# Squares moved to ScalarE, VectorE's order written out and a third weight's low part made by DMA, in the first stage of a two-layer decoder trunk

## The chip, the cores and the metric

The kernel runs on one core of one Trainium2 chip. The time is device microseconds (us) for one execution of the whole program; three executions of the kernel before took 2656.12, 2658.39 and 2658.79 us, median 2658.39. Engine names as in the profile: PE is TensorE (matrix multiply) and PEld its weight load, DVE is VectorE, ACT is ScalarE, POOL is GpSimd, SP is SyncE, whose queue issues most DMA transfers.

## The reference, cut to what matters

Two layers (`DEPTH = 2`) of a hybrid block on one sequence of 1024 tokens of width 1024, all in float32:

```python
for l in range(DEPTH):
    h = rmsnorm(x, norm_mix[l])
    proj = einsum('btd,de->bte', h, w_in[l])
    q, k, v, u, ug, ga, gb = split(proj, SPLITS, axis=-1)   # 1024, 128, 128, 512, 512, 1024, 1024 wide
    a_out = sliding_window_attention(partial_rope(rmsnorm(q)), partial_rope(rmsnorm(k)), v, sinks[l])
    c_out = conformer_conv(u, ug, ...)        # GLU, causal depthwise convolution of width 31, LayerNorm, silu, projection
    x = x + (sigmoid(ga) * a_out + sigmoid(gb) * c_out) @ w_out[l]
    g, up = split(rmsnorm(x, norm_ffn[l]) @ w_gate_up[l], 2)
    x = x + (silu(g) * up) @ w_down[l]
```

## The kernel before, in words

The activations lie transposed: 8 tiles of 128 channels x 1024 tokens. Each float32 operand of a matrix product is split in two numbers, a rounded high part (`hx`, `wh`) and the low rest (`lx`, `wl`), and a product is the three terms `wh*hx + wh*lx + wl*hx` (`mm3`, L245 to L251). A term on 1024 tokens is a pair of matmuls of 128x512. One k-step of one weight tile is three such pairs, in the order hx,wh, then lx,wh, then hx,wl, so the low part of the weight is wanted only by the third pair.

RMSNorm is not applied to the input before the product. The tile x is scaled by the norm's weight and split (`split_g`: ACT makes `hx`, DVE makes `lx`), and the factor per token, 1/rms, is multiplied into the results later. For it, the squares of the 8 input tiles are added up in `acc` (`sumsq`), a row of 16 tiny matmuls (`tokmean`, `pss` in the rows) sums `acc` over channels, POOL raises to the power -1/2 (`rtok`), DVE spreads it on a diagonal (`dg`) and two matmuls (`pb`) broadcast it to the tile `R`.

The first stage of a layer projects K and V together (8 k-steps of six pairs), then `u0`, the first convolution tile (third weight), then `ug0`, `q0` and so on in the order of `INPROJ`. In layer 1 (`l == 0`) the program starts with nothing on the chip: the eight input tiles `xi` and the weights arrive by DMA during the K and V steps. In layer 2 the input is already split when K and V begin.

Weights are fetched ahead by `fetch`: a DMA on SP's queue brings the raw tile, ACT casts it to `wh` (L134), `low` makes `wl`. There are two ways for that. While `spaced[0]` is false, POOL subtracts, `wl = raw - wh` (L141). When it is true, ACT writes `wl = -wh` (L144) and an accumulating DMA on POOL's queue adds the weight from memory to it (L145). `spaced[0]` is set after the K and V steps. Tiles of `wl` come from two buffers (`WLO = 2`), so the third weight's `wl` takes the buffer of the first one (K's).

The order of PE's instructions is the order of the code (`MAN`). DVE's is that of the code from the K results on (`dve`); in the head of the program the order on ACT, DVE and POOL is chosen by a list scheduler from its estimate of times. Pending pieces such as `norm_a` are placed by a clock of k-steps (`after`, `tick`): in layer 1 `norm_a` comes two ticks after the K and V loop, which is after the first k-step of `u0`; in layer 2 it comes before it.

The convolution's tile `y` (L510) is 128x1024 float32 with one buffer; it is first written when `ug0` is done.

## Time and profile before

| | us |
|---|---|
| median of three executions (lowest, highest) | 2658.39 (2656.12, 2658.79) |
| the profiled execution | 2658.14 |
| its span, first to last instruction | 2656.4 |
| PE busy in the span | 2562.6 (96%) |
| DVE, POOL, ACT busy | 1785.8, 1423.7, 1152.9 |
| mean granted clock of PE | 0.987 |

The span is cut into stages by times from its start: in layer 1, K and V run from 7.2 to 34 us and u0 from there to 63 us; in layer 2, K and V run from 1343 to 1365 us. A row of the timeline gives start, duration, engine, line, operation, what it writes and reads, and in brackets how long the engine had been idle and what ended that. Busy POOL and DVE times hold waits for each other, as two durations of one instruction show, for instance 1.89 and 2.87 us for the same square.

### The profile page before, as it was taken

The page shows a single profiled execution, that of the slowest core. Times are in us where ns is not written, and L with a number is a line of the kernel's source. Part 1 is how long each engine was busy: PE and PEld are TensorE (multiplying, and loading weights), DVE is VectorE, ACT ScalarE, POOL GpSimd, SP SyncE. Part 2 cuts the span into 40 slices and gives each one's busy share as a digit, 9 for nine tenths or more (in the row PEclk, how much of TensorE's full clock was granted, in tenths as well). Part 3 has the DMA queues.
Part 4 walks back from the last instruction along what each step waited for, and adds up shares of the span by engine and source line. Part 5 has one row for each costly group of instructions (what it writes and reads, how often), then busy time and mean ns, then how long its engine had stood idle before and what let it go on. Part 6 is the DMA issues. An engine that isn't in the chain of part 4 may idle for free.

```text
span 2656.4 us, 33362 instructions
## 1 busy us (share of the span) xinstructions
PE 2562.6 (96%) x11736; PEld 2094.6 (79%) x11736; DVE 1785.8 (67%) x2063; ACT 1152.9 (43%) x2290; POOL 1423.7 (54%) x1004
## 2 busy tenths in 40 slices
PE   7998999999999999999999989999999999999999
PEld 5786877888778888878777778778887788888887
DVE  6688988551667777855637989975516777878344
ACT  3365666632523222344524656666225223233443
POOL 6165565325257767765522655653253667777444
PEclk8999999999999999999999999999999999999999
DMA  4444345675254444476734444456733454446666
GB/s 150 95 100 121 97 107 136 182 248 206 95 182 149 160 167 169 159 275 217 236 96 93 111 111 102 110 148 212 258 143 119 163 178 159 151 167 218 212 226 208
DMA packets 146119, 427.30 MB, mean 161 GB/s; under 512 B 17120, under 2 KB 17376, under 8 KB 145952
## 3 DMA queue, kind: packets, MB, share of 16 engines
q1 hardware_dynamic: 137168, 393.63, 44.0%
q0 software_dynamic: 8640, 31.46, 7.0%
q8 instruction: 92, 1.51, 0.2%
q14 instruction: 75, 0.61, 0.1%
q10 hardware_dynamic: 144, 0.09, 0.0%
HBM read 290.63 MB, written 115.34 MB: 153 GB/s over the span
## 4 chain that ended last, share of the span: by engine, by line
PE 69%; DVE 13%; DMA 6%; ACT 4%; issue 3%; POOL 3%; SPq 1%; DVEq 0%; ACTq 0%; POOLq 0%
PE b L873 43%; PE ps L251 21%; DVE y L515 5%; DMA qs<-q 2%; DMA rot<-q 1%; PE po L721 1%; POOL rot L398 1%; PE pT L691 1%; ACT wh L134 1%; DVE q L412 1%; DVE acc L304 1%; POOL q L397 1%; DMA yd<-y 1%; DVE A L733 1%; DVE mx L671 1%
## 5 line engine op out<-in xcount | busy, mean ns | idle before, releaser
L160 POOL TENSOR_TENSOR plo<-fraw,phi 128x512 fp32r<-128x512 f32 x290 | 425.4, 1476 | 232.8 <-ACT phi L158 219.4
L160 POOL TENSOR_TENSOR plo<-fs,phi 128x512 fp32r<-128x512 f32 x160 | 262.4, 1650 | 252.2 <-ACT phi L158 244.3
L515 DVE SCALAR_TENSOR_TENSOR y<-a,vec,y 128x1024 f32<-128x1024 f32 x240 | 358.4, 1493 | 3.8
L158 ACT CAST phi<-fraw 128x512 fp32r<-128x512 f32 x444 | 257.6, 618 | 235.0 <-POOL plo L160 134.5
L251 PE MATMUL ps<-hx,wh 128*128 128x512 f32 x1056 | 343.2, 406 | 7.2 <-ACT hx L292 7.2
L251 PE MATMUL ps<-hx,wl 128*128 128x512 f32 x1056 | 331.9, 395 | 6.0 <-POOL wl L141 6.0
L251 PE MATMUL ps<-lx,wh 128*128 128x512 f32 x1056 | 332.7, 396 | 0.8 <-DVE lx L293 0.8
L158 ACT CAST phi<-fs 128x512 fp32r<-128x512 f32 x160 | 95.4, 620 | 534.1 <-DVE fs L173 534.1
L160 DVE TENSOR_TENSOR plo<-fraw,phi 128x512 fp32r<-128x512 f32 x154 | 129.4, 847 | 188.7 <-ACT phi L158 186.5
L873 PE MATMUL b<-plo,phi 128*128 128x512 f32 x616 | 240.6, 391 | 5.3 <-DVE plo L160 5.1
L251 PEld LDWEIGHTS ps<-hx,wl 128*128 128x128 f32 x1056 | 201.4, 191 | 50.1 <-POOL wl L141 6.5
L873 PE MATMUL b<-phi,plo 128*128 128x512 f32 x616 | 239.8, 389 | 0.0
L873 PE MATMUL b<-phi 128*128 128x512 f32 x616 | 239.7, 389 | 0.0
L251 PEld LDWEIGHTS ps<-lx,wh 128*128 128x128 f32 x1056 | 202.4, 192 | 47.0 <-DVE lx L293 2.2
L251 PEld LDWEIGHTS ps<-hx,wh 128*128 128x128 f32 x1056 | 191.1, 193 | 42.1 <-ACT hx L292 7.2
L141 POOL TENSOR_TENSOR wl<-raw,wh 128x1024 fp32r<-128x1024 f32 (+1 forms) x40 | 79.9, 1998 | 192.7 <-PE ps L251 176.4
L675 ACT ACTIVATE sc<-sc,nm,fq 128x129 f32<-128x129 f32 x256 | 123.7, 487 | 117.5 <-DVE nm L673 117.2
L134 ACT CAST wh<-raw 128x1024 fp32r<-128x1024 f32 (+1 forms) x100 | 98.0, 980 | 164.8 <-PE ps L251 113.3
L937 DVE TENSOR_TENSOR g<-g 128x512 f32<-128x512 f32 x88 | 105.0, 1193 | 66.4 <-POOL g L941 46.2
L145 POOL DMA_DIRECT2D wl<-win x60 | 53.3, 888 | 177.6 <-ACT wl L144 172.6
L706 POOL TENSOR_SCALAR_AFFINE_SELECT ph<-ph 128x512 fp32r<-128x512 f32 x64 | 69.3, 1083 | 143.0 <-DVE pl L698 143.0
L941 POOL TENSOR_TENSOR g<-g,u 128x512 f32<-128x512 f32 (+1 forms) x84 | 128.6, 1548 | 30.6 <-DVE u L994 24.2
(254 smaller groups left out, 6184.5 us busy)
## 6 DMA issues: line engine op xcount, KB each, us to landing
fraw<-wgu SPq DMA_DIRECT2D x88, 512.0 KB
raw<-win SPq DMA_DIRECT2D x68, 512.0 KB
wl<-win POOLq DMA_DIRECT2D x60, 512.0 KB, 6.4
act<-g SPq DMA_DIRECT2D x44, 512.0 KB
dw<-wdn SPq DMA_DIRECT2D x44, 512.0 KB
td<-g SPq DMA_DIRECT2D x44, 512.0 KB
sd<-dw SPq DMA_DIRECT2D x44, 512.0 KB
fraw<-sd SPq DMA_DIRECT2D x88, 256.0 KB
```

Of the source, the lines that this page charges most:

```text
L134: nc.scalar.copy(wh, raw)
L141: nc.gpsimd.tensor_tensor(out=wl, in0=raw, in1=wh.bitcast(F32), op=ALU.subtract)
L145: nc.gpsimd.dma_start(wl, src, accum_op=ALU.add)
L158: nc.scalar.copy(hi, src)
L160: (eng or nc.gpsimd).tensor_tensor(out=lo, in0=src, in1=hi.bitcast(F32), op=ALU.subtract)
L251: nc.tensor.matmul(ps[:, sl], a[:, wc], b[:, sl], start=first and j == 0, stop=last and j == 2)
L515: nc.vector.scalar_tensor_tensor(out=y, in0=a[:, j:j + T], scalar=V(w0 + j), in1=y, op0=ALU.mult, op1=ALU.add)
L675: nc.scalar.activation(sc[:, n], sc[:, n], AF.Exp, bias=nm[:, n:n + 1], scale=fq[:, 4 * j + n:4 * j + n + 1], accum_out=den[:, n:n + 1])
L706: nc.gpsimd.affine_select(out=src, in_=src.bitcast(F32), pattern=[[0, 4], [-1, P]], compare_op=ALU.is_gt, fill=0.0, base=0, channel_multip ...
L873: nc.tensor.matmul(ps, w[:, ai * P:(ai + 1) * P], x, start=first and j == 0, stop=last and j == 2, skip_group_check=True)
L937: nc.vector.tensor_tensor(out=o, in0=x, in1=y, op=ALU.subtract)
L941: nc.gpsimd.tensor_tensor(out=g[:, sl], in0=g[:, sl], in1=u[:, sl], op=ALU.mult)
```

## The change

Four edits in the head of the program, two of which also hold in layer 2.

1. The squares of the eight input tiles in layer 1 are made by ACT (`AF.Square`) and no longer by POOL; the additions into `acc` stay on DVE.
2. The order on DVE and ACT in the head is that of the code: split of tile e, then square and addition of tile e - 1. The first two weights' high and low parts are made inside that loop (`parts` holds them back until then).
3. `spaced[0]` becomes true before the third weight is prepared, in both layers, so its low part is made by ACT and the accumulating DMA.
4. That low part lies in a tile of the convolution's tag `y` (`spare`), in both layers, and no longer in K's `wl` buffer; the first weight whose `wl` waits for the buffer of one that is used after V is now the sixth, and no longer the fifth. `YB = 1` only names the number of `y` buffers.

```diff
-    def fetch(limit=len(wseq)):
+    spare = []
+
+    def fetch(limit=len(wseq), parts=len(wseq)):
...
-        while given[1] < given[2] and given[1] <= given[0] + AHEAD:
+        while given[1] < min(given[2], parts) and given[1] <= given[0] + AHEAD:
...
-            wl = wp.tile([P, n], F32R, tag="wl", bufs=WLO, name="wl")
+            wl = spare.pop() if spare else wp.tile([P, n], F32R, tag="wl", bufs=WLO, name="wl")
...
-    def sumsq(acc, x, e, first=False, add=None):
+    def sumsq(acc, x, e, add=None):
         sq = acc if e == 0 else t4("sq")
-        if first:
-            nc.gpsimd.tensor_tensor(out=sq, in0=x, in1=x, op=ALU.mult)
-        else:
-            nc.scalar.activation(sq, x, AF.Square)
+        nc.scalar.activation(sq, x, AF.Square)
         if e > 0:
             (add or nc.gpsimd).tensor_tensor(out=acc, in0=acc, in1=sq, op=ALU.add)
...
             with tc.manual_schedule(engines={mybir.EngineType.SP}):
-                fetch(1)
+                fetch(1, 0)
                 for e in range(KD):
                     nc.sync.dma_start(xin[e], xT[e])
                     if e == 0:
-                        fetch(2)
+                        fetch(2, 0)
                 nc.sync.dma_start(vec[1], vecs[1])
-            for e in range(KD):
-                x = xin[e]
-                xs.append(split_g(x, V(V_GM + e), f"x{e}"))
-                sumsq(acc, x, e, True, nc.vector)
+            with tc.manual_schedule(engines={mybir.EngineType.DVE, mybir.EngineType.Activation}):
+                for e in range(KD):
+                    if e < 2:
+                        fetch(2, e + 1)
+                    xs.append(split_g(xin[e], V(V_GM + e), f"x{e}"))
+                    if e > 0:
+                        sumsq(acc, xin[e - 1], e - 1, nc.vector)
+                sumsq(acc, xin[KD - 1], KD - 1, nc.vector)
             ins.close()
...
-        wk, wv = next_w(), next_w()
+        wk = next_w()
+        spaced[0] = True
+
+        spare.append(ap_.tile([P, T], F32R, tag="y", bufs=YB, name="wl"))
+        wv = next_w()
...
-        spaced[0] = True
         keys(psk)
```

What this does to the order of POOL in the head of layer 1, from the first weight's low part on (`wl`, `raw`, `wh` are weight tiles, `xi` the input tiles, `acc` and `sq` the squares, `rot` and `a` tiles that are cleared). Before:

```order
L141 TENSOR_TENSOR wl<-raw,wh 128x1024
L300 TENSOR_TENSOR acc<-xi_111 128x1024
L141 TENSOR_TENSOR wl<-raw,wh 128x1024
L300 TENSOR_TENSOR sq<-xi_112 128x1024
...
L300 TENSOR_TENSOR sq<-xi_118 128x1024
L377 MEMSET rot 128x1024
L493 MEMSET a 128x30 x2
L141 TENSOR_TENSOR wl<-raw,wh 128x1024
L145 DMA wl<-win 128x1024
L314 TENSOR_TENSOR rtok<-rse,mhalf 128x8
```

and now:

```order
L143 TENSOR_TENSOR wl<-raw,wh 128x1024 x2
L380 MEMSET rot 128x1024
L496 MEMSET a 128x30 x2
L147 DMA wl<-win 128x1024 x2
L313 TENSOR_TENSOR rtok<-rse,mhalf 128x8
L400 TENSOR_TENSOR k_354<-k_354,ct 128x1024
```

The eight squares and the third subtraction are gone from POOL; the third and the fourth weight's accumulating DMAs stand ahead of `rtok`.

ACT in the same place, from the second input tile on, now (`hx` is the high part of an input tile, L136 the cast of a weight; before, the seven `hx` stood in a row, the cast of the third weight behind them and no square or `wl` among them):

```order
L294 ACTIVATE hx_149<-xi_112,vec_95 128x1024
L301 ACTIVATE acc<-xi_111 128x1024
L294 ACTIVATE hx_154<-xi_113,vec_95 128x1024
L301 ACTIVATE sq<-xi_112 128x1024
...
L136 CAST wh<-raw 128x1024
L294 ACTIVATE hx_189<-xi_118,vec_95 128x1024
L301 ACTIVATE sq<-xi_117 128x1024
L301 ACTIVATE sq<-xi_118 128x1024
L146 ACTIVATE wl<-wh 128x1024
L136 CAST wh<-raw 128x1024
L424 ACTIVATE k_354<-ps,vec_95 128x1024
```

Seven `hx`, eight squares and a cast now stand between the second input tile's arrival and the third weight's `wl<-wh`, which came behind the K results before.

DVE in the head, now (`lx` is the low part of an input tile):

```order
L295 SCALAR_TENSOR_TENSOR lx_150<-xi_112,vec_95,hx_149 128x1024
L295 SCALAR_TENSOR_TENSOR lx_155<-xi_113,vec_95,hx_154 128x1024
L303 TENSOR_TENSOR acc<-acc,sq 128x1024
L295 SCALAR_TENSOR_TENSOR lx_162<-xi_114,vec_95,hx_161 128x1024
L303 TENSOR_TENSOR acc<-acc,sq 128x1024
...
L295 SCALAR_TENSOR_TENSOR lx_190<-xi_118,vec_95,hx_189 128x1024
L303 TENSOR_TENSOR acc<-acc,sq 128x1024 x2
L312 TENSOR_SCALAR rse<-pss 128x8
```

Low parts and additions alternate from the third tile on, and two additions are left at the end; before, five stood behind the last low part.

Elsewhere PE's order is the same instruction for instruction. On SP the fifth weight's raw tile is fetched one place earlier in both layers, in layer 1 ahead of the tables `ct` and `st_`. Two places away from the head moved too: once in the middle of layer 1 a weight's cast and `wl<-wh` on ACT stand ahead of four softmax scalings (L682) and no longer behind them, and two neighbours on DVE in the feed-forward part (L931, L994) change places.

More of the change, by code (lines that the diff above doesn't have):

```diff
@@ L509, in conv_taps @@
                 w0 = V_CWT + c * CW
-                y = ap_.tile([P, T], F32, tag="y", bufs=1, name="y")
+                y = ap_.tile([P, T], F32, tag="y", bufs=YB, name="y")
                 nc.vector.tensor_scalar(out=y, in0=a[:, 0:T], scalar1=V(w0), scalar2=V(V_CB + c),
@@ L586, in out @@
                     load(c + 2)
-            s2 = ap_.tile([P, T], F32, tag="y", bufs=1, name="s2")
+            s2 = ap_.tile([P, T], F32, tag="y", bufs=YB, name="s2")
             load(0)
@@ L895, in trunk @@
                                                op0=ALU.mult, op1=ALU.subtract)
-            sumsq(acc, x, e, False, nc.vector if e == KD - 1 else None)
+            sumsq(acc, x, e, nc.vector if e == KD - 1 else None)
         xst.close()
@@ L1168 @@
 TD, AD = 7.5, 5.5
+YB = 1
 S0 = 16
```

## The prediction

> **What bounds the kernel now.** I read the page's busy times first, then the head in windows, PE's timeline, and what PE's waits end on.
>
> ```profile
> PE 2562.6 (96%) x11736; PEld 2094.6 (79%) x11736; DVE 1785.8 (67%) x2063; ACT 1152.9 (43%) x2290; POOL 1423.7 (54%) x1004
> 35.40:41.40 6.00, 0.01 (x1) 0.00 (x0) 5.79 (x3) 1.11 (x1) 5.20 (x5) 0.84 0.16 65
> 41.40:47.40 6.00, 4.77 (x19) 4.05 (x19) 2.29 (x2) 2.90 (x3) 1.06 (x1) 0.50 0.55 123
> 47.40:53.00 5.60, 5.60 (x15) 4.34 (x15) 3.75 (x3) 0.00 (x0) 5.28 (x3) 0.50 0.75 171
> 54.00:60.00 6.00, 6.00 (x33) 4.80 (x32) 0.17 (x1) 0.59 (x1) 2.46 (x2) 1.00 0.00 0
> ```
>
> A window row gives length, then busy time of PE, PEld, DVE, ACT and POOL, then PE's granted clock. PE is the bound overall, and it stands still from 35.4 to 41.4 us. Behind the hole its clock is granted at 0.50 until 53 us, so the hole costs more than its length.
>
> ```profile
> 11.99 0.74 PE L251 MATMUL psv<-lx,wh 128*128 128x512 f32 x2
> 14.33 0.73 PE L251 MATMUL psv<-hx,wl 128*128 128x512 f32 x2 [1.59 <-POOL wl L141]
> 14.90 0.62 PE L251 MATMUL ps<-hx,wh 128*128 128x512 f32 x2
> 25.79 0.62 PE L251 MATMUL ps<-hx,wh 128*128 128x512 f32 x2
> 34.34 0.61 PE L251 MATMUL ps<-hx,wh 128*128 128x512 f32 x2
> 34.80 0.61 PE L251 MATMUL ps<-lx,wh 128*128 128x512 f32 x2
> 41.44 1.22 PE L251 MATMUL ps<-hx,wl 128*128 128x512 f32 x2 [6.03 <-POOL wl L141]
> 43.85 3.58 PE L308 MATMUL pss<-onesD,acc 128*128 128x1 f32 x16 [1.19 <-DVE acc L304]
> 47.29 1.20 PE L251 MATMUL ps<-hx,wh 128*128 128x512 f32 x2
> 54.23 1.02 PE L326 MATMUL pb<-dg,onesmat 128*128 128x512 f32 x2
> 65.97 0.61 PE L436 MATMUL ptk<-ident,k 128*128 128x128 f32 x4
> ```
>
> These are, in order: V's last two pairs of step 0; K's step 1 and step 5 (four steps in 10.89 us, 2.72 each); u0's three pairs; `tokmean`; u0's step 1; the first broadcast; K's transposition, from which point layer 1 has nothing of the head left. PE waits three times: for V's low weight, for u0's low weight, for `acc`. All three come from the order on POOL and DVE:
>
> ```profile
> 39.04 2.35 POOL L141 TENSOR_TENSOR wl<-raw,wh 128x1024 fp32r<-128x1024 f32 x1
> L300 POOL TENSOR_TENSOR sq<-xi x7: 1892/2870/2872, 14.2 to 36.2; 128x1024 f32<-128x1024 f32 x7
> L304 DVE TENSOR_TENSOR acc<-acc,sq x9: 1214/2909/3206, 20.9 to 2008.8; 128x1024 f32<-128x1024 f32 x9
> L293 DVE SCALAR_TENSOR_TENSOR lx<-xi,vec,hx x8: 1271/2461/3386, 7.2 to 29.0; 128x1024 fp32r<-128x1024 f32 x8
> ```
>
> The third subtraction starts on POOL at 39.04, behind the last square. The squares and DVE's work hold each other up: a square takes 1.89 us or 2.87, an addition 1.21 or 2.9, a low part 1.27 or more (least, median, most, in ns).
>
> **The change, part by part.**
>
> *The K and V stage.* V's low part no longer stands behind a square. The first subtraction ends at 8.12 (5.77 + 2.35) and DVE's low part, which waited for it, at 9.21 (7.20 + 2.01):
>
> ```profile
> 5.77 2.35 POOL L141 TENSOR_TENSOR wl<-raw,wh 128x1024 fp32r<-128x1024 f32 x1 [2.91 <-ACT wh L134]
> 7.20 2.01 DVE L293 SCALAR_TENSOR_TENSOR lx<-xi,vec,hx 128x1024 fp32r<-128x1024 f32 x1 [7.20 <-ACT hx L292]
> 9.34 7.55 ACT L292 ACTIVATE hx<-xi,vec 128x1024 fp32r<-128x1024 f32 x6 [0.23 <-DMA xi<-xT]
> ```
>
> V's subtraction then runs 9.21 to 11.56, and PE's pair follows the one at 11.99 by a pair's 0.46 (34.34 to 34.80), at 12.45 in place of 14.33. Step 1 starts at 12.90 and seven steps of 2.72 end at 31.95, where u0 began at 34.34: 2.39 us gained. This needs ACT and DVE to keep up: ACT's period is 1.15 + 1.06 (below) = 2.21, DVE's 1.27 + 1.21 = 2.48, both under 2.72, with a lead of one step at the start (the second low part is done by 12.8, wanted at 13.4). If DVE's period were over 2.72 the excess would be paid seven times.
>
> *The hole.* What ends it is the landing of the new DMA.
>
> ```profile
> L292 ACT ACTIVATE hx<-xi,vec x8: 1147/1150/1152, 6.0 to 17.1; 128x1024 fp32r<-128x1024 f32 x8
> L302 ACT ACTIVATE sq<-xa x14: 1042/1061/1062, 616.7 to 2002.2; 128x1024 f32<-128x1024 f32 x14
> 43.42 1.05 ACT L144 ACTIVATE wl<-wh 128x1024 fp32r<-128x1024 f32 x1
> 44.37 1.03 ACT L134 CAST wh<-raw 128x1024 fp32r<-128x1024 f32 x1
> 44.79 1.06 POOL L145 DMA_DIRECT2D wl<-win  x1 [3.40 <-ACT wl L144]
> DMA to landing us min/median/max: 5.3/6.4/9.9
> ```
>
> Neighbours on ACT start 0.10 closer than they last (0.95 for 1.05). From the second tile's start at 9.34: seven `hx` at 1.05, eight squares at 0.96 and a cast at 0.95 are 15.98 us, so `wl<-wh` runs 25.32 to 26.37. The squares' buffers do not hold ACT up: each waits for an addition some three tiles back. POOL is idle and issues 0.32 later (44.47 to 44.79), at 26.7; the median landing of 6.4, over all 60 such DMAs, gives 33.1. u0's third pair is due at 31.95 + 0.92 = 32.87, so the hole shrinks from 6.19 us (41.44 less 35.25) to 0.23: 5.96 gained. The bounds: without overlap on ACT the issue is at 28.3. Landings then lie between 26.7 + 5.3 = 32.0 (no hole, 0.2 more gained) and 28.3 + 9.9 = 38.2 (a hole of 5.3). I take 33.1, since the overlap is seen here and the median holds DMAs issued among loads and busy DVE.
>
> *Clock and `acc`.* ACT's last square ends at 25.3 and DVE's additions, even at 2.48 a step from 11.56, at 28.9; `acc` is wanted at 33.6, so that wait goes. With no hole the clock stays, as it did over the wait of 1.59 us. Layer 2 shows the same work at full clock:
>
> ```profile
> 1364.92 1.84 PE L308 MATMUL pss<-onesD,acc 128*128 128x1 f32 x16
> 1366.62 0.71 PE L251 MATMUL ps<-hx,wh 128*128 128x512 f32 x2
> 1370.80 1.02 PE L326 MATMUL pb<-dg,onesmat 128*128 128x512 f32 x2
> ```
>
> From third pair to `tokmean` 0.46 in place of 2.41: 1.95 gained. `tokmean` 1.70 in place of 3.44: 1.74. Three steps to the broadcast 4.18 in place of 6.94: 2.76. The broadcast needs `dg`:
>
> ```profile
> 49.43 3.41 DVE L319 TENSOR_TENSOR dg<-ident,rtok 128x1024 f32<-128x1024 f32 x1 [1.58 <-POOL rtok L314]
> 1369.20 1.23 DVE L319 TENSOR_TENSOR dg<-ident,rtok 128x1024 f32<-128x1024 f32 x1 [1.93 <-POOL rtok L314]
> 1348.70 0.63 ACT L1088 ACTIVATE x<-x 128x512 f32<-128x512 f32 x1 [3.06 <-DMA xn<-x]
> 1363.13 1.11 ACT L421 ACTIVATE k<-ps,vec 128x1024 f32<-128x1024 f32 x1
> 1369.70 2.96 POOL L397 TENSOR_TENSOR k<-k,ct 128x1024 f32<-128x1024 f32 x1 [0.54 <-issue]
> ```
>
> Before, POOL's rope product came first and `dg` ended at 52.84, 5.4 after `tokmean`, hidden by the slow clock. In layer 2 `dg` came first and ended at 1370.43, in time. Now the rope needs K's copy on ACT (31.95 less half a step is 30.6; a cast, then the copy, to about 32.8) and its DMAs: in layer 2 it begins 5.5 us after that copy (1364.24 to 1369.70), so here at 38.3. `dg` begins, as in layer 2, 2.6 after `tokmean` (1366.62 to 1369.20), which ends at 35.3: at 37.9, so it goes first. I take no wait; the margin is 0.4 us, and if `tokmean` slips by more the order turns and 1.2 us is paid (5.4 after `tokmean` against 4.2).
>
> *The rest.* From 54.23 to 65.97 PE ran at full clock, so this shifts as a whole. The `y` tile is written by the convolution only after `ug0`: nothing. The fetch ahead of `ct` and `st_` holds them to about 22 us, wanted at 38. In layer 2 the low part's -wh follows ACT's last square at 1349.3 and lands by 1357 (at most 1361), wanted at 1367.5 (1366.62 and two pairs); POOL's subtraction there was hidden too, by V's last steps. Nothing either way, with over 6 us of cover; what a later landing exceeds it by would be paid in full. On ACT in the middle of layer 1 a cast and a -wh (1.05 + 1.06) move once ahead of four softmax scalings: at most 2.0 us if PE waits for these; I take 0, since PE reaches their transpositions only behind six pairs of its own, and 0 for DVE's two neighbours.
>
> The sum: 2.39 + 5.96 + 1.95 + 1.74 + 2.76 = 14.8 us, K's transposition at 51.2. From the profiled execution's 2658.14 (span 2656.4) this is 2643.3; the median lies 0.25 higher, so **2643.5**. How stiffly the rest follows is seen where both layers run the same program:
>
> ```profile
> 525.66 150.94 PE ps L251 x660
> 1842.07 150.94 PE ps L251 x660
> 1383.90 0.28 PE L436 MATMUL ptk<-ident,k 128*128 128x128 f32 x1
> ```
>
> From K's transposition to the long run of matmuls it is 459.7 us in layer 1 and 458.2 in layer 2: I allow 3 us for that.
>
> **A rule against it.** The landing times above are those of DMAs issued while DVE was mostly busy. The Trainium skill, page SBUF — State Buffer, section SBUF: two separate sides, says that a DMA issued from POOL's queue can be blocked until a DVE instruction that holds the shared port ends, because POOL cannot write the descriptors. By that rule the issue would wait for the last addition at about 28.0. No row here shows such a block by itself. What that would cost is the second rival's smaller price.
>
> **The rivals.**
>
> *The DMA lands late.* For it: DVE is busy until 28, and the longest landing is 9.9. Against: the median of 60. If the issue waits for DVE until 28.0, landing is at 34.5: a hole of 1.6 and 1.2 for `dg`, 2646.3. At 26.7 + 9.9 = 36.6 the hole is 3.7: with `dg` 2648.2; if the clock halves too, the third pair (0.5), 1.74 and 2.76 come back in place of `dg`'s wait, 2652.0. Page TensorE: Matmul & The Clock Gate of the Trainium skill, section What's actually happening, sets the limit at an idle window of about 3.4 us; the traces agree that 1.59 does not and 6.03 does halve it.
>
> *Given back later.* The in-projection of layer 1 waits in places for DMA and DVE. If these do not shift with PE, up to half the gain is lost, 7 us: 2650.5. Against: all of them start from u0's and K's results.
>
> *ScalarE becomes the bound of the head* (the other side). If a square on ACT here takes s from start to start, the DMA lands at 25.4 + 8s, and everything else of the hole stays cold. At s = 2.15 u0's third pair is at 42.6 and `tokmean` where it was; beyond that the change is slower, and at POOL's 2.87 the landing is 48.4 and the time 2664. Against: 1.06 in L302's row, same size.
>
> *The change does nothing.* If ACT's -wh still waited for a buffer that K frees, the hole would stay: 2658. The new tile has no earlier user.
>
> **How the numbers follow.** My forecast 0.62; late DMA 0.20; given back 0.12; ScalarE 0.03; nothing 0.03. A measurement of this kernel tells 0.2% (5.3 us) from no change: below 2653.1 is faster. That takes in the first three but for about 0.02 of their ends: faster 0.92, same 0.05, slower 0.03. The range: the forecast less the 3 us of stiffness and 0.5 for earlier landings, 2640, up to the middle of the late and given-back cases, 2651.
>
> **What would show it.** PE's hole before u0's third pair under 1 us and ended by a DMA; u0's first pair near 32.0; `acc` complete by 29; clock 1.00 from 30 to 54; K's transposition near 51.2; `dg` of 1.2 us; layer 2 unchanged. Wrong, if ACT's -wh ends after 28, if the landing takes over 8 us, if the clock falls before `tokmean`, or if K's transposition moves and the long run of matmuls (525.66) does not.

## The result, and the profile after

The changed kernel takes 2643.77 us (median of four executions, 2642.37 to 2647.37); the kernel before, beside it on the same chip, 2657.26 (2653.95 to 2658.79). The ratio is 0.9948, 95% interval 0.9933 to 0.9964: faster, by 13.5 us or 0.5%. The profiled execution took 2642.97 us, with a span of 2641.3 and a mean granted clock of 0.992.

Windows of the changed kernel, with the columns of the prediction's first fence; the last row is the whole stretch:

```profile
35.40:41.40 6.00, 6.00 (x26) 4.53 (x26) 1.56 (x3) 1.77 (x3) 5.60 (x4) 1.00 0.84 186
...
30.00:54.00 24.00, 22.53 (x116) 18.19 (x115) 6.68 (x10) 8.15 (x9) 11.81 (x6) 1.00 0.55 126
```

Where PE stood still from 35.4 to 41.4 us it is now busy throughout, and the granted clock is 1.00 from 30 to 54 us. (The 1.47 us that PE lacks in the last row are a wait that ends at 53.5 us, behind K's first transposition; the kernel before has it too, up to 68.1 us.) The timeline of PE in the head, the same instructions as in the prediction's second fence:

```profile
12.72 0.63 PE L253 MATMUL psv<-hx,wl 128*128 128x512 f32 x2
13.19 0.62 PE L253 MATMUL ps<-hx,wh 128*128 128x512 f32 x2
...
32.24 0.62 PE L253 MATMUL ps<-hx,wh 128*128 128x512 f32 x2
...
33.15 0.63 PE L253 MATMUL ps<-hx,wl 128*128 128x512 f32 x2
33.62 1.84 PE L307 MATMUL pss<-onesD,acc 128*128 128x1 f32 x16
35.32 0.71 PE L253 MATMUL ps<-hx,wh 128*128 128x512 f32 x2
...
39.59 1.02 PE L325 MATMUL pb<-dg,onesmat 128*128 128x512 f32 x2
...
51.45 0.60 PE L439 MATMUL ptk<-ident,k 128*128 128x128 f32 x4
```

No row has a wait in brackets: the three waits of the kernel before (1.59, 6.03 and 1.19 us) are gone. K's transposition stands at 51.45 us instead of 65.97, so the head has gained 14.5 us. The engines that fed those waits, in the same view:

```profile
25.04 1.05 ACT L146 ACTIVATE wl<-wh 128x1024 fp32r<-128x1024 f32 x1
...
25.33 2.55 DVE L303 TENSOR_TENSOR acc<-acc,sq 128x1024 f32<-128x1024 f32 x2
...
26.41 1.06 POOL L147 DMA_DIRECT2D wl<-win  x1 [4.01 <-ACT wl L146]
...
37.74 1.23 DVE L318 TENSOR_TENSOR dg<-ident,rtok 128x1024 f32<-128x1024 f32 x1 [1.87 <-POOL rtok L313]
...
38.10 3.11 POOL L400 TENSOR_TENSOR k<-k,ct 128x1024 f32<-128x1024 f32 x1 [0.40 <-DMA rot<-k]
```

The accumulating DMA is issued at 26.41 and has landed when PE wants it at 33.15; `acc` is complete at 27.9; `dg` starts 0.36 us ahead of the rope product on POOL and takes 1.23 us.

Between the head and the end the gain shifts by up to 3 us either way. From the two timelines:

| stretch | before | after | gained |
|---|---|---|---|
| start to layer 1's K transposition | 65.97 | 51.45 | 14.5 |
| from there to layer 1's feed-forward `pss` | 627.8 | 625.6 | 2.2 |
| from there to layer 2's first K pair | 649.4 | 648.9 | 0.5 |
| from there to layer 2's `pssl` (end of the convolution) | 468.4 | 471.5 | -3.2 |
| from there to the end | 844.9 | 843.9 | 1.1 |

The loss in the fourth row has a place of its own, which the experiments found.

### The profile page after: what moved, and what is told of

The parts are those of the page before. It is cut to its first block, busy times and chain, and to the rows that moved or that the text cites. A ratio compares the mean times of both kernels' runs of the same rounds, so it can differ in the third digit from the quotient of the medians.

```text
span 2641.3 us, 33363 instructions
## 1 busy us (share of the span) xinstructions
PE 2554.7 (97%) x11736; PEld 2089.6 (79%) x11736; DVE 1767.1 (67%) x2063; ACT 1161.9 (44%) x2300; POOL 1398.8 (53%) x996
## 4 chain that ended last, share of the span: by engine, by line
PE 36%; DVE 6%; DMA 3%; ACT 2%; POOL 2%; issue 2%; SPq 0%; DVEq 0%; ACTq 0%; POOLq 0%
PE b L879 23%; PE ps L253 10%; DVE y L518 2%; DMA qs<-q 1%; DMA rot<-q 1%; POOL plo L162 1%; DMA yd<-y 0%; PE po L724 0%; PE psv L253 0%; POOL rot L401 0%; ACT wh L136 0%; PE pT L694 0%; DVE q L415 0%; ACT sc L678 0%; POOL q L400 0%
## 5 line engine op out<-in xcount | busy, mean ns | idle before, releaser
L143 POOL TENSOR_TENSOR wl<-raw,wh 128x1024 fp32r<-128x1024 f32 (+1 forms) x38 | 74.3, 1957 | 174.7 <-PE ps L253 134.7
L136 ACT CAST wh<-raw 128x1024 fp32r<-128x1024 f32 (+1 forms) x100 | 98.1, 981 | 152.8 <-PE ps L253 121.5
```

The lines of the kernel that those rows point to most:

```text
L136: nc.scalar.copy(wh, raw)
L143: nc.gpsimd.tensor_tensor(out=wl, in0=raw, in1=wh.bitcast(F32), op=ALU.subtract)
```

## The experiments

All times are medians; "before" is the kernel before, run beside it on the same chip. The profiles' K transposition in layer 1 stands beside each.

| run | us | before | ratio (95% interval) | K transposition |
|---|---|---|---|---|
| low part by subtraction on POOL | 2641.86 | 2657.56 | 0.9944 (0.9929 to 0.9959) | 53.01 |
| DMA into K's tile | 2662.22 | 2657.56 | 1.0020 (1.0008 to 1.0031) | 61.44 |
| DMA and its tile alone | 2660.74 | 2657.56 | 1.0017 (1.0008 to 1.0026) | 67.12 |
| no written order | 2655.38 | 2657.56 | 0.9997 (0.9987 to 1.0008) | 60.84 |
| no written order, root put back | 2645.31 | 2660.04 | 0.9948 (0.9934 to 0.9962) | 51.78 |
| DMA 3 us later | 2652.03 | 2660.04 | 0.9972 (0.9959 to 0.9985) | 58.27 |
| warm start, 24 | 2649.35 | 2660.04 | 0.9961 (0.9949 to 0.9973) | 51.06 |
| warm start, low part on POOL | 2647.89 | 2660.04 | 0.9956 (0.9941 to 0.9970) | 52.89 |
| the changed kernel again | 2647.42 | 2657.97 | 0.9964 (0.9951 to 0.9978) | 52.90 |
| low part on POOL again | 2645.16 | 2657.97 | 0.9949 (0.9936 to 0.9961) | 52.97 |
| warm start, 20 | 2648.06 | 2657.97 | 0.9965 (0.9954 to 0.9976) | 50.95 |
| `dg` behind the product | 2652.40 | 2657.97 | 0.9976 (0.9964 to 0.9987) | 54.59 |

### Is it the DMA, or POOL without the squares?

From the changed kernel, edits 3 and 4 undone in both layers:

```diff
-        wk = next_w()
-        spaced[0] = True
-        spare.append(ap_.tile([P, T], F32R, tag="y", bufs=YB, name="wl"))
-        wv = next_w()
+        wk, wv = next_w(), next_w()
...
+        spaced[0] = True
         keys(psk)
```

> The changed kernel with its last two edits undone in both layers: the third weight's low part is again a subtraction on GpSimd, into the tile that K's low part leaves, and the convolution's tile is not used for it. The squares stay on ScalarE and the written order stays. Nothing is left out of the computation. Theory (GpSimd, rid of the squares, is what mattered): K's tile comes free when K's last matmul pair ends, at about 30.9 us; 2.35 us of subtraction (the row of the kernel before) give 33.3, up to 33.8 with VectorE beside it (2.87 us, the dearest square); the pair that reads it is due at 33.15. So a hole of 0.1 to 0.7 us, the first K transposition at 51.5 to 52.2 (51.45 in the changed kernel), and 2643.9 to 2644.5 us in all. Rival (the accumulating DMA into a tile of its own is what closed the hole): the hole stays at over 2 us, the transposition comes later than 54 us, and the time is 2647 us or more.

The timeline of that kernel:

```profile
32.35 2.39 POOL L143 TENSOR_TENSOR wl<-raw,wh 128x1024 fp32r<-128x1024 f32 x1 [10.17 <-PE ps L253]
...
34.79 0.73 PE L253 MATMUL ps<-hx,wl 128*128 128x512 f32 x2 [0.41 <-POOL wl L143]
35.36 1.84 PE L307 MATMUL pss<-onesD,acc 128*128 128x1 f32 x16
```

POOL, idle for 10.17 us, subtracts as soon as PE has left K's tile, and PE waits 0.41 us. The time is that of the changed kernel, and below it rather than above. The theory holds: edits 1 and 2 carry the gain, and the DMA in a tile of its own saves 0.41 us in the head. The transposition is later than forecast for another reason: all of PE's work from 14 us on is 1.1 us later, since PE's pairs were still 1.05 us long until about 14.7 us instead of 12.3 (see below).

The opposite test is the kernel before with edits 3 and 4 alone, `spaced[0] = True` and the `spare` tile ahead of the second `next_w()`.

> The kernel before with only the last two edits of the change: the accumulating DMA for the third weight's low part, and the convolution's tile for it. The squares stay on GpSimd and the scheduler sets the order. Nothing is left out of the computation. Theory (the edits hang together: the squares hold GpSimd's queue, and the DMA is issued from there): the last square and the fills end at 39.0 us as before, the DMA is issued then and lands 5.3 to 6.4 us later, at 44.4 to 45.5, where the subtraction had ended at 41.4. The hole grows from 6.03 to 9.0 to 10.1 us; the sum of squares is done at 43.8 either way, so its wait (1.19 us) goes and tokmean begins 1.9 to 2.9 us later than at 43.85. 2660 to 2661 us, slower than the kernel before. Rival (the DMA and its tile carry the gain of the hole by themselves): no hole before the third pair, 2652 us or less.

Its timeline:

```profile
31.92 9.98 DVE L306 TENSOR_TENSOR acc<-acc,sq 128x1024 f32<-128x1024 f32 x5
...
39.10 1.06 POOL L147 DMA_DIRECT2D wl<-win  x1
...
44.84 1.22 PE L253 MATMUL ps<-hx,wl 128*128 128x512 f32 x2 [9.32 <-DMA wl<-win]
```

The DMA is issued behind POOL's last square and fills, as the subtraction was, and lands 5.74 us later; the hole grows from 6.03 to 9.32 us, and the kernel is 3.2 us slower than before. Without edit 1, edits 3 and 4 do harm. Edit 1 by itself was not run.

Then edit 3 without edit 4: the line with `spare.append` taken out, so that the DMA goes into K's tile. (In this run and two below, a manual order on POOL around `norm_a` and `rope` keeps `rtok` ahead of the rope products.)

> The changed kernel with its accumulating DMA, but into the tile that K's low part leaves instead of the convolution's tile (the spare tile undone, in both layers). GpSimd's order at the head (the reciprocal root before the rotation's product) is written down as the changed kernel has it, so that it doesn't move. Nothing is left out of the computation. Theory (a late DMA is paid in full, and the clock on top of it): ScalarE's -wh can't begin before K's last pair ends at 30.9 and stands behind the copy of the fourth weight (30.67 to 31.7), so it ends at 32.8; GpSimd issues until 33.9, and the landing comes 5.3 to 6.4 us after the issue began at 32.8 to 32.9, at 38.2 to 39.3. The pair is due at 33.15: a hole of 5.0 to 6.1 us. As after the kernel before's hole of 6.03 us the granted clock falls to half for some 10 us: tokmean 3.58 instead of 1.84, three steps 6.94 instead of 4.18, another 4.5 us. Together 2653.3 to 2654.4 us. Rival (the clock fell in the kernel before for another reason than the hole, such as the late sum): the hole alone, 2648.8 to 2649.9 us, with a clock of 1.00 all through.

```profile
33.64 1.06 POOL L148 DMA_DIRECT2D wl<-win  x1 [11.24 <-ACT wl L147]
...
39.52 1.22 PE L254 MATMUL ps<-hx,wl 128*128 128x512 f32 x2 [5.89 <-DMA wl<-win]
40.53 3.40 PE L308 MATMUL pss<-onesD,acc 128*128 128x1 f32 x16
...
1364.23 1.22 PE L254 MATMUL ps<-hx,wl 128*128 128x512 f32 x2 [3.02 <-DMA wl<-win]
```

In layer 1 all went as expected: hole 5.89 us, half clock behind it (`tokmean` 3.40), transposition at 61.44. The last addition to `acc` ended at 27.9 there, so the clock fell behind the hole and not for a late sum. But the time is 8 us over the forecast, because the same wait stands in layer 2 too, which the forecast left out: there ACT's -wh waits for K's tile as well, the hole is 3.02 us and half clock follows. From K's first pair to K's transposition layer 2 takes 46.0 us, where the changed kernel takes 41.0. Another 5.6 us come after that, up to `pssl`, spread over the waits of the attention; these I did not trace. So edit 3 needs edit 4, and both need edit 1.

### What the written order does

The changed kernel without its `manual_schedule` on DVE and ACT in the head:

> The changed kernel without the written order of VectorE and ScalarE at the head: the scheduler sets it. All else stays, and nothing is left out of the computation. The scheduler then puts three squares ahead of the scaled copies that feed TensorE, and on GpSimd the two products of K's rotation ahead of the reciprocal root. Theory: the K and V stage keeps its pace (the last scaled copy ends at 25.2 instead of 23.2, wanted with its low part at 29.9), u0's third pair starts at 33.1 to 33.4, but the reciprocal root waits behind 4.7 us of GpSimd products that begin at 38.1: it ends at 44.5, dg at 45.1 to 45.7, where the broadcast wants it at 39.6. A new hole of 5.5 to 6.1 us ahead of the broadcast, and since it is as long as the 6.03 us after which the clock fell in the kernel before, up to 4.5 us at half clock: 2649 to 2654.5 us. Rival (only the engine that takes the squares matters, not the order): 2643 to 2645 us, no hole over 1 us before 50 us.

```profile
38.86 2.37 POOL L400 TENSOR_TENSOR k<-k,ct 128x1024 f32<-128x1024 f32 x1 [2.13 <-DMA rot<-k]
...
43.50 1.67 POOL L313 TENSOR_TENSOR rtok<-rse,mhalf 128x8 f32<-128x8 f32 x1
...
45.20 1.23 DVE L318 TENSOR_TENSOR dg<-ident,rtok 128x1024 f32<-128x1024 f32 x1 [8.58 <-POOL rtok L313]
46.48 2.07 PE L325 MATMUL pb<-dg,onesmat 128*128 128x512 f32 x2 [5.98 <-DVE dg L318]
```

The hole has moved from the third pair to the broadcast, 5.98 us long, and the broadcast behind it takes 2.07 instead of 1.02 us: half clock. Nearly all of the gain is gone (the time is 0.9 us above the range expected), though the squares are on ACT and the DMA lands in time. The scheduler, left to itself, puts `rtok` behind the rope products on POOL. With only that put back (POOL's order written around `norm_a` and `rope`, ACT and DVE still the scheduler's):

> The run without the written order, with one thing put back: on GpSimd the reciprocal root is again ahead of the two products of K's rotation, as in the changed kernel. The scheduler still sets VectorE and ScalarE at the head. Nothing is left out of the computation. Theory (of the written order, what counts is that the root keeps its place): the hole of 5.98 us ahead of the first broadcast goes, and with it the half clock behind it; the first K transposition comes at 51.5 to 53.0 us, as in the two kernels that have the order written, and the time is 2642 to 2645 us. Rival (the order of the squares and copies itself costs the time): a hole of over 3 us stays before 56 us, in the K and V stage or ahead of tokmean, and the time stays above 2649 us.

```profile
36.10 1.94 POOL L314 TENSOR_TENSOR rtok<-rse,mhalf 128x8 f32<-128x8 f32 x1
...
39.94 1.02 PE L326 MATMUL pb<-dg,onesmat 128*128 128x512 f32 x2
```

The broadcast waits for nothing: `rtok` is made ahead of the rope product again, and the time is the changed kernel's. So the scheduler's order on ACT and DVE is as good as the written one. What edit 2 is worth, 9 us of the head (60.84 against 51.78), comes through POOL, an engine whose order it does not write.

### A late transfer, and the margin of `dg`

The changed kernel with three more squares on ACT ahead of the -wh:

```diff
                 sumsq(acc, xin[KD - 1], KD - 1, nc.vector)
+                for _ in range(3):
+                    nc.scalar.activation(xin[KD - 1], xin[KD - 1], AF.Square)
```

> The changed kernel with three more squares of the last x tile, in place, on ScalarE between its last square and its -wh; nobody reads them, and nothing is left out of the computation. GpSimd's order at the head is written down as the changed kernel has it. ScalarE's -wh begins 3.0 us later, at 28.0, ends at 29.1, GpSimd issues at 29.3 to 29.4. The two other kernels that waited for this transfer had it 5.7 and 5.9 us after the issue began, so it lands at 35.0 to 35.3; the pair is due at 33.2 to 34.3 (by when the clock rises at the start). Theory (a DMA that is late costs its lateness and no more, as long as the hole stays short): a hole of 0.7 to 2.1 us, granted clock 1.00 behind it, tokmean 1.84 us; sum and root are late by as much and hide; the first K transposition at 52.2 to 54.6, and 2644.0 to 2646.5 us in all. Rival (even a short hole halves the clock, as the hole of 3.02 us in layer 2 did where the DMA went into K's tile): tokmean 3.4 us, the next three steps 6.9 us, 2649 us or more.

Its timeline, and behind it a window row:

```profile
30.03 1.06 POOL L148 DMA_DIRECT2D wl<-win  x1 [7.62 <-ACT wl L147]
...
35.83 0.72 PE L254 MATMUL ps<-hx,wl 128*128 128x512 f32 x2 [1.60 <-DMA wl<-win]
36.39 1.84 PE L308 MATMUL pss<-onesD,acc 128*128 128x1 f32 x16
...
40.17 2.69 POOL L406 TENSOR_TENSOR k<-k,ct 128x1024 f32<-128x1024 f32 x1
40.54 5.73 DVE L319 TENSOR_TENSOR dg<-ident,rtok 128x1024 f32<-128x1024 f32 x1 [1.90 <-POOL rtok L314]
...
42.52 2.66 POOL L407 TENSOR_TENSOR rot<-rot,st__208 128x1024 f32<-128x1024 f32 x1
...
46.32 1.12 PE L326 MATMUL pb<-dg,onesmat 128*128 128x512 f32 x2 [2.25 <-DVE dg L319]
```

```profile
38.00:42.00 4.00, 4.00 (x13) 3.19 (x13) 1.80 (x3) 0.00 (x0) 4.00 (x3) 0.57 0.85 202
```

Neither theory was right as it stood. The hole was 1.60 us, inside the forecast, and `tokmean` kept its 1.84 us. But the clock fell after `tokmean` (0.57 from 38 to 42 us), and `dg` came behind the rope product: it took 5.73 us, until both products were done, and the broadcast waited 2.25 us more. K's transposition is 5.4 to 6.8 us later than in the two profiles of the changed kernel (52.90 and 51.45), and of the gain over the kernel before 8.0 us are left. The transfer was issued 3.5 to 3.6 us later than in those two profiles (30.03 against 26.55 and 26.41); 2 us of that were hidden, and the other 1.6 cost more than three times their length.

To price the margin of `dg` by itself, the changed kernel with the first half of `dg` computed once more ahead of the whole (`twice` is true in layer 1):

```diff
         dg = t4("dg")
+        if twice:
+            nc.vector.tensor_tensor(out=dg[:, 0:HALF]..., in0=ident..., in1=r[:, 0:NB // 2]..., op=ALU.mult)
```

> The changed kernel with the first half of dg (the diagonal matrix for the broadcast, VectorE) computed twice, once by itself and then with the whole: 0.6 us more on VectorE between the root and dg, so that the whole dg begins at 38.4 us, behind GpSimd's product k·ct (38.1) and not 0.4 us ahead of it. Nothing is left out of the computation. Theory (VectorE's elementwise work stands while GpSimd's runs): dg takes 3.4 to 5.7 us instead of 1.23, ends at 41.8 to 44.1, the broadcast that is due at 39.6 waits 2.2 to 4.5 us, and if the clock falls behind it another 1.7 to 3.4: 2646 to 2651.5 us. Rival (the price of the lost margin is 1.2 us, as the prediction took it): the broadcast waits 0.3 to 1.3 us, 2644 to 2645.2 us.

```profile
39.00 2.51 POOL L404 TENSOR_TENSOR k<-k,ct 128x1024 f32<-128x1024 f32 x1 [0.44 <-DMA rot<-k]
39.33 3.28 DVE L322 TENSOR_TENSOR dg<-ident,rtok 128x1024 f32<-128x1024 f32 x1
41.48 3.35 POOL L405 TENSOR_TENSOR rot<-rot,st__205 128x1024 f32<-128x1024 f32 x1
42.66 1.13 PE L329 MATMUL pb<-dg,onesmat 128*128 128x512 f32 x2 [2.04 <-DVE dg L322]
```

Here `dg` began 0.33 us behind the product, stood until that was done, and got its turn ahead of the second product, which then took 3.35 us instead of 2.35. The broadcast waited 2.04 us and the clock held. The wait is just under the theory's 2.2 to 4.5, and well over the rival's 1.3. The median, 2652.40, is 5 us above the changed kernel's on the same chip, of which the trace puts only these 2 us down to `dg`; it is also 0.9 above the range expected, and where the rest comes from stays open. So the price of the lost margin is 2.0 us where `dg` comes between the products, and more where it comes behind both; it is not 1.2.

### The start at half speed

The changed kernel's first pairs on PE take 1.05 to 1.22 us, later ones 0.62; this is called half speed here. When it ends differs from profile to profile of the same instructions: at 12.3 us in the changed kernel, at 15.6 in its second run.

> The changed kernel itself, once more, beside the runs of this call. Nothing is left out of the computation. Theory: about 0.5% faster than the kernel before on the same chip, the ratio within 0.9935 to 0.9962, the transfer of the third weight's low part hidden again. TensorE's change to full speed at the start has come anywhere from 12.3 to 14.7 us in seven profiles of kernels without a warm start, so the first K transposition may come at 51.4 to 52.7 us.

The second run's timeline:

```profile
14.65 1.04 PE L253 MATMUL ps<-lx,wh 128*128 128x512 f32 x2
15.51 0.66 PE L253 MATMUL ps<-hx,wl 128*128 128x512 f32 x2
```

u0's first pair is at 33.71 instead of 32.24, and K's transposition 1.45 us later. Both that transposition (52.90) and the ratio, 0.9964, are just outside what was expected; between the two runs the kernel's gain is 10.5 and 13.5 us, with intervals that overlap.

Three kernels give PE unread work at the very start, so that the slow time passes before the first weights are there: the changed kernel with 24 and with 20 such matmuls, and the kernel with the low part on POOL with 24:

```diff
+        if l == 0:
+            warm = psm.tile([P, HALF], F32, tag="pT", bufs=1, name="warm")
+            for _ in range(24):
+                nc.tensor.matmul(warm[:, 0:P], onesmat, onesmat, start=True, stop=True)
```

> The changed kernel with 24 matmuls of 128x128 on the matrix of ones, into an otherwise idle PSUM tile, at the very start of TensorE's work; their result is not read, and nothing is left out of the computation. Theory (the first matmuls run at half speed because TensorE has just begun, whatever it computes): TensorE is busy from about 1.5 us, and the first step's matmuls at 9.3 us take 0.62 us instead of 1.05 to 1.22. Step 1 then waits for V's low part (GpSimd, 11.5 us) and begins at 11.9 to 12.4, not 13.19; all that follows TensorE's pace comes 0.8 to 1.3 us earlier than in the changed kernel (up to 2.4 us against a run where full speed came late). u0's third pair is then due at 31.9 to 32.4, and a transfer of 5.7 to 5.9 us from 26.4 lands at 32.1 to 32.3: a hole of at most 0.4 us. The first K transposition at 50.2 to 50.9, 2641.5 to 2643.2 us in all. Rival (the slow start is a fixed time after the launch or comes with the loading of the tiles): step 1 at 13.2 or later, no gain.

> The changed kernel with 20 unread matmuls of 128x128 at the start of TensorE's work instead of the 24 that ran until 9.3 us. Nothing is left out of the computation. At 168 ns for each half, as there, 40 halves take 6.7 us and end at 8.0, before VectorE hands over the first low part at 9.2. Theory: the first step runs at full speed from 9.3 us, step 1 begins at 12.0 to 12.3 (13.19 in the changed kernel, 12.63 with 24), the first K transposition comes at 50.2 to 50.7, and the median lies 0.5 to 2 us under the changed kernel's on the same chip; so small a gain may not show. Rival: the transfer of the third weight's low part, due 1 us earlier, is late and costs 0.3 us or more, and if the clock falls for it another 1.7 to 3.4 us.

> Both the warm start (24 unread matmuls at the start of TensorE's work) and the third weight's low part by subtraction on GpSimd into K's tile, in both layers. Nothing is left out of the computation. The subtraction follows K's last pair, so its hole stays at 0.4 to 0.5 us wherever TensorE stands; the first K transposition, 53.01 us in the kernel without the warm start, comes 1.3 to 2.5 us earlier, at 50.5 to 51.7. If both effects add up, 2639.5 to 2641.5 us, the fastest of these kernels; if the difference of 2 us between the kernel with the subtraction and the changed one is only what the rest of the program gives and takes from one execution to the next, 2641 to 2643 us.

The timeline of the kernel with 20:

```profile
7.79 0.71 PE L253 MATMUL ps<-hx,wh 128*128 128x512 f32 x2
...
12.45 0.63 PE L253 MATMUL ps<-hx,wh 128*128 128x512 f32 x2
```

The head does nearly what the theory says: short pairs from the first, step 1 at 12.45 and, with 24, at 12.63, K's transposition at 50.95 and 51.06 (each under 0.3 us later than expected), and no wait for the transfer, which is wanted 0.4 to 0.6 us earlier than in the changed kernel's first profile. In the times nothing is seen of it. With 20 it is 2648.06 against 2647.42 for the changed kernel on the same chip; with 24 it is 2649.35, 10.7 us below the kernel before beside it, where 2641.5 to 2643.2 was expected. A gain of 0.5 to 2 us in the head is less than what the rest of the program gives and takes.

The third kernel shows how near its limit the low part on POOL is. Its hole is the same 0.41 us as without the warm start, but the clock fell behind it:

```profile
32.84 0.73 PE L253 MATMUL ps<-hx,wl 128*128 128x512 f32 x2 [0.41 <-POOL wl L143]
...
35.30 1.20 PE L253 MATMUL ps<-hx,wh 128*128 128x512 f32 x2
```

`dg` then came behind the product as well, by 0.04 us (it took 3.44), and the transposition stands at 52.89, no earlier than without the warm start. In the two runs with the subtraction and without the warm start `dg` had gone first by only 0.15 and 0.03 us. So the two do not add up, and the time, 2647.89, is 5 us above what was expected at most.

### What edits 3 and 4 cost in layer 2

> The kernel with the third weight's low part by subtraction on GpSimd into K's tile, once more, to be held against the changed kernel on the same chip. Nothing is left out of the computation. Theory (the DMA and its tile carry none of the gain): the two medians lie within 2 us of each other, either way. Rival (the DMA or the shared tile costs something later in the program, where the earlier run of this kernel was 2 us faster though its head was 1.6 us slower): this one is faster again by 1.5 us or more.

On one chip the kernel with the subtraction takes 2645.16 us and the changed kernel 2647.42; earlier, on different chips, it was 2641.86 and 2643.77. Both times it is 2 us faster by the medians, but the intervals overlap, so the times alone do not settle it. The traces show a place. In the changed kernel's first profile, near the end of layer 2's convolution:

```profile
1743.64 2.40 POOL L400 TENSOR_TENSOR q<-q,ct 128x1024 f32<-128x1024 f32 x1 [4.30 <-DMA rot<-q]
1743.73 2.32 DVE L676 TENSOR_TENSOR nm<-mx,nfq 128x4 f32<-128x4 f32 x1
...
1755.68 1.26 ACT L685 ACTIVATE sc<-sc,ri 128x128 f32<-128x128 f32 x4
...
1756.11 1.35 PE L694 MATMUL pT<-ident,sc 128*128 128x128 f32 x4 [2.63 <-ACT sc L685]
```

The same place with the subtraction, second run:

```profile
1743.31 2.94 POOL L400 TENSOR_TENSOR q<-q,ct 128x1024 f32<-128x1024 f32 x1 [2.10 <-DMA rot<-q]
...
1755.89 1.26 ACT L685 ACTIVATE sc<-sc,ri 128x128 f32<-128x128 f32 x4
...
1756.32 1.21 PE L694 MATMUL pT<-ident,sc 128*128 128x128 f32 x4 [0.97 <-ACT sc L685]
```

The last q tile's rotation waits for its four small transfers, and in the changed kernel they land some 2 us later. On the first product hangs a chain: POOL's second product, DVE's sum of the two (`q<-q,rot`), ACT's copy of it, three more pieces on ACT, and only then the softmax's scaling `sc`, which PE's transpositions read. From DVE's sum to `sc` it is 7.24 us in the changed kernel and 7.25 in the other. So `sc` is late with the product, and PE waits 2.63 us instead of 0.97. DVE's `nm`, a 128x4 operation that starts just behind the product and takes 2.32 us, is not the cause: in the kernel without written order, root put back, it came ahead of the product and took 0.16 us, and PE waited all the same:

```profile
1745.16 0.16 DVE L685 TENSOR_TENSOR nm<-mx,nfq 128x4 f32<-128x4 f32 x1
...
1757.84 1.35 PE L703 MATMUL pT<-ident,sc 128*128 128x128 f32 x4 [2.95 <-ACT sc L694]
```

The wait is not the whole cost. Behind it the granted clock falls, in the changed kernel to 0.50 (the first number behind POOL's):

```profile
1758.00:1760.00 2.00, 2.00 (x9) 1.81 (x9) 1.31 (x4) 0.93 (x2) 0.48 (x2) 0.50 1.01 270
```

From these transpositions to the next matmuls with `meanmat` (`pmu`) it takes 6.17 us there, and 4.71 with the subtraction, where the clock stays at 1.00. In all ten profiles of kernels with the accumulating DMA for the third weight POOL waits 3.9 to 4.6 us at this place, PE waits 2.2 to 3.0, and the clock falls to about half (5.7 to 6.3 us to `pmu`); in all four without it (before, both runs with the subtraction, and the third warm one) it is 2.1 to 2.3, 1.0, and no fall (4.7). From layer 2's first K pair to `pssl` the former take 471.0 us or more, the latter 468.4, 469.2, 468.1 and, once, 472.3. So the changed kernel gains 0.4 us in the head by edits 3 and 4, and loses 1.7 us of waiting and 1.5 at half clock here, together the 3.2 us in the fourth row of the table of stretches.

Why the small transfers land later stays open: around them SP's queue has the same order in both kernels. One thing goes with it in the traces. In each of the ten, one or two packets of a DMA queue that the profile calls `q14 instruction` fall 2.5 to 3.5 us behind the issue of the raw weight's fetch that precedes the small transfers, and the first small transfer is issued 1.4 us behind that fetch; in the four there is no such packet, and it is 1.1 us. Whether that packet or the added transfers delay them, no run tells.

## Why the prediction was right, point by point

The mechanism held: POOL rid of the squares, three waits gone, the clock kept. That the median came within 0.3 us of the forecast is luck. The same kernel's second run gave 2647.42; the kernel before took 2657.26 beside the changed one, and not the 2658.39 that the forecast took off from; and behind the head 3.8 us were gained and 3.2 lost, which are no terms of the forecast. Against the kernel before, 14.9 us were forecast and 13.5 and 10.5 measured.

| step of the prediction | forecast | measured |
|---|---|---|
| u0's first pair | 31.95 | 32.24 |
| -wh on ACT ends; DMA issued | 26.37; 26.7 | 26.09; 26.41 |
| hole ahead of the third pair | 0.23 | 0 |
| third pair to `tokmean` | 0.46 | 0.47 |
| `tokmean` to the next step | 1.70 | 1.70 |
| three steps to the broadcast | 4.18 | 4.27 |
| `acc` complete | 28.9 | 27.9 |
| `dg`, rope product begin | 37.9, 38.3 | 37.7, 38.1 |
| K's transposition | 51.2 | 51.45 |
| gained in the head | 14.8 | 14.5 |
| median | 2643.5 | 2643.8 |

- *K and V stage: 2.39 forecast, 2.10 measured, and not a fixed number.* The cause is right, but the size was taken from a kernel in which it was hidden: before, the half speed ended at about 12.3 us inside the wait for V's low part (until 14.33), so its end did not matter. With the wait gone, u0 starts at 32.24 where full speed comes at 12.3 and at 33.71 where it comes at 15.6: against the one profile of the kernel before this term is 0.6 or 2.1 us, by chance.
- *Hole: 5.96 forecast, 6.18 measured* (third pair 6.64 us behind the second before, 0.46 now). The landing was put at 33.1, from the median of 6.4 us. Where PE waited for this same transfer, it came 5.74, 5.88 and 5.80 us after the issue began (the kernels with the DMA alone, into K's tile, and 3 us later), which is an estimate of 32.2 for the changed kernel: near the lower bound, 0.9 us ahead of need. ACT's overlap of neighbours held.
- *Clock and `acc`: as forecast*, each of the three differences within 0.1 us; `acc` was done 1 us earlier, since a step of DVE took 2.33 us for 2.48. The order of `dg` and the product went as forecast too, with a margin of 0.36 us for 0.4.
- *The price behind that margin was wrong.* "1.2 us is paid" took POOL's product to delay `dg` by the difference of two older rows. It is 2.0 us when `dg` gets in between the two products and 4.5 us of `dg` (5.73 for 1.23) when it does not. It did not matter here, since the margin held.
- *The late DMA* would have been worse than its middle case. That rival charged 1.6 us of hole and 1.2 for `dg`, 2.8 together. With a hole of just 1.60 us the run's head lost 5.4 to 6.8 us, near the 8.5 set for a hole of 3.7 us with half clock. The step that failed is "the traces agree that 1.59 does not and 6.03 does halve it": a hole of 1.59 between pairs of 128x512 did not, but 1.60 followed by `tokmean` did. The length of about 3.4 us that the prediction cites as the limit was no safe one here.
- *The rule against it did not show.* By the Trainium skill, page SBUF — State Buffer, section SBUF: two separate sides, an operation of DVE in its two-port mode can keep POOL from writing the descriptors of its DMA; the prediction extended this to DVE's additions. With the DMA alone, DVE was busy from 31.92 to 41.90 us over an issue at 39.10, and the landing took 5.74 us; into K's tile, with DVE idle, 5.88. For these operations of DVE (float32 additions of two tiles) the trace shows no such block.
- *Given back later: the 3 us of stiffness were needed.* Layer 1 gave 2.2 us more and layer 2 took 3.2. "Layer 2: nothing either way" was right for the low part itself (there PE waits for nothing), and wrong for the convolution's end, where the kernels with the transfer lose some 3 us. The prediction has no term for that place.
- *ScalarE as the bound, and no effect*, did not come near: ACT's period was 1.99 us (the square at 1.04 and the copy at 1.15 overlap), PE's step 2.72.

What the prediction did not see is which edits matter. It gave the hole to the accumulating DMA; a subtraction on a free POOL closes it as well, all but 0.41 us. And it gave the written order no term of its own, though without it 9 us of the head are lost, on POOL.

## What to carry to other kernels

When a queue is rid of work, ask for each later instruction on it whether the old way would now be in time: here the plain subtraction was, 0.41 us short, and the kernels with the new transfer lost some 3 us elsewhere, for a reason that stays open. When a scheduler's order is replaced on some engines, compare the order on the engines that are not written too; here 9 us hung on the order of three instructions on a third engine. A margin of 0.4 us between two engines that stand still for each other should be priced at the whole length of what would go first, and a hole of a few microseconds, or a shorter one next to thin matmuls, at the hole plus a fallen clock.

## What the runs showed of the hardware that I had not expected

- The half speed at the start ends at no fixed time after PE begins. Its first matmul is at 7.2 to 7.5 us in all eleven profiles without a warm start, and the pairs become short anywhere from 12.2 to 15.6 us. The Trainium skill, page TensorE: Matmul & The Clock Gate, section What's actually happening, says that the gate's window of about 3.4 us runs freely and does not start with the kernel; the spread of 3.4 us agrees with that, but not with the ±500 ns that the same section gives for it.
- The granted clock in the windows does not show this. In the changed kernel, where pairs take 1.05 to 1.22 us, the window's clock (the last but two of its numbers) is 1.00:

```profile
7.00:12.00 5.00, 3.94 (x8) 2.65 (x9) 3.62 (x2) 4.04 (x5) 3.57 (x2) 1.00 1.02 416
```

- The clock can fall behind a hole of 0.41 us if `tokmean`'s 16 matmuls of 128x1 follow (the third warm kernel), and did not behind the same rows in the two other runs with the subtraction. Holes of 1.60 and 3.02 us were each followed by some 3.5 to 4 us at half speed, and the clock fell likewise behind all ten waits of 2.2 to 3.0 us at the end of layer 2's convolution. It did not fall behind the 2.04 us ahead of the broadcast in the kernel with `dg` behind the product. So its length alone does not tell whether a hole lowers the clock.
- A DVE operation that starts 0.1 to 0.4 us behind one of POOL's stands until that is done: `dg` of 1.23 us took 3.28 in one kernel, and 5.73 in another, where POOL's next product got ahead of it. Even a 128x4 operation took 2.32 us, where it took 0.16 ahead of the product.
